# Grouping a burst's PSUM banks by their reader, and moving the norms' scalings behind dense products, in a gated HGRN2 and retention layer

## The chip, the cores and the metric

The kernel runs on one core of a Trainium2 chip. A core has five engines that run side by side, each with its own in-order queue: TensorE (PE in the profile, its weight loads PEld), VectorE (DVE), ScalarE (ACT), GpSimd (POOL) and SyncE (SP, which issues DMAs). Matmul results go to PSUM, eight banks of 128 partitions by 512 floats; the rest is in SBUF. The metric is the device time of one execution in microseconds, less is better.

## The reference

One decoder layer over 2048 positions of width 1024, in fp32. `h` is an adaptive RMS norm of `x`, one projection makes ten column groups, two recurrences run on them, their outputs are normed per head, gated and summed, and an output projection and a last norm follow:

```python
h = rms_norm(x, norm_g) * (1 + scale) + shift
hq, hf, hi, hz, rq, rk, rv, rz, ga, gb = split(h @ w_in)
oA = hgrn2_chunkwise(hq, hf, hi, lower_bounds)     # 8 heads, dk = dv = 128
uA = head_rms_norm(oA, hg_norm_g) * silu(hz)
oB = retention_chunkwise(rotary(rq), rotary(rk), rv)  # 8 heads, dk = 64, dv = 128
uB = head_rms_norm(oB, ret_norm_g) * silu(rz)
m = sigmoid(ga) * uA + sigmoid(gb) * uB
out = rms_norm(x + gate * (m @ w_out), final_g)
```

HGRN2 is `S_t = diag(f_t) S_{t-1} + (1 - f_t) i_t^T`, `o_t = S_t^T q_t` with a gate per channel; retention has one constant decay per head. Both are computed in chunks of 128 positions: a part inside the chunk (a masked score matrix times the values) and a part from the state, which every chunk updates.

## The kernel before

**Dense products.** The sequence is taken in two halves of 1024 positions. The input projection is cut into 36 quads per half (`ORDER`: a and v for HGRN2, b for retention's q and k, A and B for the gates), and each quad is seven products of a Strassen-like scheme (`product`). A product is four steps (`product_step`, j = 0 to 3) of three fp32r matmuls of 128x512. Their results lie in four PSUM banks with the tags x0, x1 and v, and are evicted by `after` at the product's end: some by ACT (`stash`, L487), some by DVE (L500 to L511). `deliver` then does the quad's own work: sigmoids, rotary (L652 to L655), gates (L693 to L707). Weights are split into two fp32r parts by ACT and DVE (L299, L300). The evictions and the splits are issued with raised priority.

**The background.** Everything else that PE does is fitted between these steps by the class `Background`. After every product step `bg.tick(1.0)` counts one tick; when eight have passed (four in one stretch of each half) `burst` advances each running generator once, in the order lanes (`hgrn_out`), rets (`retention`), trees (`tree`). `post` delays a DMA by so many ticks. `force` runs a burst at once when a tile is needed, `drain` at the end.

- `tree` builds the masked score matrix of an HGRN2 head level by level into the bank "lv" (L74 and L71), DVE multiplies factors into q and k (L814, L815, L818, L819).
- `hgrn_out` does one chunk of a head: key-value product, score times value, q times state, all into one bank "o" (`poh`, two buffers); DVE updates the state `st` from the first (L915), ACT norms the second.
- `retention` does one chunk of a pair of heads: it transposes k, multiplies the last chunk's scores with v, adds q times state, makes the next scores and the state's addition. It uses one bank "o" (`por`) and one two-bank tile "rt" (single buffer). DVE reads scores (`scm`, L1006) and state (`rs`, L1012), ACT the transposed k (`rkz`, L1009) and both outputs.
- `normed` takes the norm of an output: ACT squares with a sum (L842), POOL makes the reciprocal root (L174 or L176, then L177), ACT scales from the bank (L845). `send_u` then posts the store of u, which is fetched later for the gate, turned by PE in bank v or x (`turned_u`, the tile `uT`, L74) and multiplied (L717).

**What sets the order.** PE's instructions are pinned to program order (`InOrder`, `tc.keep_in_program_order`). For the other engines a compile-time planner picks, in simulated time, among the ready instructions the one of highest priority, which is program order except where `tc.high_priority` raises it. The order so found is each engine's queue. The planner also gives out buffers: a tile is freed when all its readers are done, and it makes accesses of one PSUM bank by different engines wait for each other in the order in which they were issued.

## Time and profile before

| What | Value |
|---|---|
| median of 3 runs (lowest, highest) | 2049.07 us (2044.88 to 2050.96) |
| the profiled execution's own time | 2047.87 us |
| its span, first to last instruction | 2046.1 us |
| PE busy | 1942.0 us, 95% |
| DVE busy | 1417.0 us, 69% |
| ACT busy | 981.2 us, 48% |
| POOL busy | 281.7 us, 14% |
| mean granted clock of TensorE | 0.987 |

A row of a group reads: line of the code, engine, operation, output and inputs by tile names, shapes, count; then busy microseconds and mean nanoseconds of one; then the idle time just before them and what ended it. A row of waits reads: who waited, for whom, microseconds in total, times, the longest. A row of a timeline reads: start, duration, engine, line, operation, tiles, count, and in brackets the idle time before and its end.

### The profile page before, as it was taken

The numbers are of one execution on the slowest core, as the hardware profiler recorded it, in microseconds if no ns is written. First come the engines' busy times: TensorE is split into PE (matmuls) and PEld (weight loads), VectorE is DVE, ScalarE is ACT, GpSimd is POOL, SyncE is SP. The second block draws the span as 40 slices with busy tenths as digits, with TensorE's granted clock in tenths as the row PEclk, the third lists the DMA queues.
The fourth block names the chain that finished last, engine by engine and source line by source line (L and its number), as shares of the span: only waits on it lengthen the run. The fifth ranks groups of instructions, "written<-read, shape, count | busy, mean of one in ns | idle before, by whom it ended". The sixth has DMA issues, their size and how long they took to land.

```text
span 2046.1 us, 40140 instructions
## 1 busy us (share of the span) xinstructions
PE 1942.0 (95%) x15172; PEld 1587.0 (78%) x15172; DVE 1417.0 (69%) x2677; ACT 981.2 (48%) x2426; POOL 281.7 (14%) x522
## 2 busy tenths in 40 slices
PE   5789899998999999999999899998999999999998
PEld 4667788877788778877888788887788878887887
DVE  6785767676767767677987676677767675868332
ACT  5524444554555446445635444534454445455331
POOL 2002110121012200201002110211011201010000
PEclk9889999999999999999999999999999999999999
DMA  8335424354353555446545424354434433246542
GB/s 296 73 89 131 123 76 113 91 140 117 106 161 117 138 138 161 148 146 200 147 109 132 124 72 109 101 148 137 115 100 126 119 86 112 73 127 191 162 144 82
DMA packets 453120, 259.96 MB, mean 127 GB/s; under 512 B 171712, under 2 KB 406208, under 8 KB 452928
## 3 DMA queue, kind: packets, MB, share of 16 engines
q1 hardware_dynamic: 286752, 172.89, 30.0%
q10 hardware_dynamic: 153120, 76.04, 13.3%
q0 software_dynamic: 13056, 8.47, 1.6%
q8 instruction: 120, 1.97, 0.4%
q14 instruction: 72, 0.59, 0.1%
HBM read 188.03 MB, written 69.21 MB: 126 GB/s over the span
## 4 chain that ended last, share of the span: by engine, by line
PE 61%; DVE 8%; DMA 7%; ACT 7%; POOL 4%; issue 3%; ACTq 1%; SPq 0%; POOLq 0%; DVEq 0%
PE x L71 25%; PE v L71 12%; PE ops L71 9%; PE y L71 6%; PE lv L71 3%; PE poh L71 2%; DVE b L300 2%; ACT b L299 2%; POOL rrh L177 1%; PE uT L74 1%; PE rt L71 1%; DVE w L425 1%; DMA wg<-in_w_gate_dram 1%; PE por L71 1%; POOL rrr L177 1%
## 5 line engine op out<-in xcount | busy, mean ns | idle before, releaser
L300 DVE TENSOR_TENSOR b<-w,b 128x512 fp32r<-128x512 f32 (+1 forms) x553 | 346.5, 634 | 291.2 <-ACT b L299 287.7
L71 PE MATMUL x<-S,b 128*128 128x512 f32 x1704 | 436.6, 401 | 9.9 <-DVE c L507 9.7
L299 ACT ACTIVATE b<-w 128x512 fp32r<-128x512 f32 (+1 forms) x553 | 316.9, 584 | 264.8 <-PE x L71 187.2
L71 PE MATMUL v<-S,b 128*128 128x512 f32 x1704 | 425.6, 398 | 4.2 <-ACT c L487 4.0
L71 PE MATMUL x<-A,b 128*128 128x512 f32 x1704 | 424.2, 397 | 3.5 <-ACT c L487 2.7
L71 PEld LDWEIGHTS v<-S,b 128*128 128x128 f32 x1704 | 317.6, 190 | 74.6 <-ACT c L487 6.4
L71 PEld LDWEIGHTS x<-A,b 128*128 128x128 f32 x1704 | 317.3, 189 | 71.4 <-ACT c L487 3.3
L71 PEld LDWEIGHTS x<-S,b 128*128 128x128 f32 x1704 | 314.9, 190 | 74.2 <-DVE c L507 7.6
L71 PE MATMUL y<-A,b 128*128 128x512 f32 x840 | 207.9, 396 | 1.9 <-DVE ro L654 1.8
L425 DVE TENSOR_TENSOR w<-w,w 128x512 f32<-128x512 f32 x284 | 194.8, 686 | 10.6 <-DMA w<-in_w_b_dram 5.4
L174 POOL TENSOR_SCALAR ssh<-ssh 128x1 f32<-128x1 f32 x128 | 49.6, 388 | 997.3 <-ACT uh L842 997.1
L71 PEld LDWEIGHTS y<-A,b 128*128 128x128 f32 x840 | 155.6, 189 | 36.2 <-issue 3.0
L71 PE MATMUL ops<-wo,m 128*128 128x512 f32 x768 | 174.5, 389 | 0.0
L71 PEld LDWEIGHTS ops<-wo,m 128*128 128x128 f32 x768 | 144.1, 188 | 29.8
L487 ACT ACTIVATE c<-v 128x512 f32<-128x512 f32 x142 | 84.6, 596 | 121.4 <-PE v L71 97.8
L845 ACT ACTIVATE uh<-poh,rrh 128x128 f32<-128x128 f32 x128 | 47.1, 368 | 154.5 <-POOL rrh L177 149.2
L71 PEld LDWEIGHTS lv<-q,k 128*32 128x32 f32 (+1 forms) x5888 | 69.8, 109 | 41.6 <-issue 30.2
L71 PE MATMUL lv<-q,k 128*32 128x16 f32 (+2 forms) x5888 | 81.0, 187 | 15.7 <-ACT af L810 5.9
L177 POOL TENSOR_TENSOR rrh<-ssh,mhalf 128x1 f32<-128x1 f32 x128 | 88.7, 693 | 10.5
L507 DVE TENSOR_TENSOR c<-c,x 128x512 f32<-128x512 f32 x71 | 48.7, 685 | 51.7 <-PE x L71 51.5
L814 DVE TENSOR_TENSOR q<-q,f 128x512 f32<-128x512 f32 x112 | 77.9, 695 | 8.2 <-PE lv L71 7.9
L815 DVE TENSOR_TENSOR k<-k,f 128x512 f32<-128x512 f32 x112 | 76.8, 686 | 0.0
(191 smaller groups left out, 2390.8 us busy)
## 6 DMA issues: line engine op xcount, KB each, us to landing
w<-in_w_d_dram ACTq DMA_DIRECT2D x128, 256.0 KB
w<-in_w_c_dram ACTq DMA_DIRECT2D x66, 256.0 KB
mu<-ud SPq DMA_DIRECT2D x64, 256.0 KB
w<-in_w_a_dram ACTq DMA_DIRECT2D x60, 256.0 KB
wa<-in_w_ada_dram SPq DMA_DIRECT2D x16, 512.0 KB
w<-in_w_b_dram ACTq DMA_DIRECT2D x32, 256.0 KB
vd<-vt SPq DMA_DIRECT2D x128, 64.0 KB
vh<-vd SPq DMA_DIRECT2D x64, 128.0 KB
```

What stands on the lines that cost most here:

```text
L71: return tc.keep_in_program_order(nc.tensor.matmul(**kw))
L74: return tc.keep_in_program_order(nc.tensor.transpose(**kw))
L174: G.tensor_scalar(out=ss, in0=ss, scalar1=n * EPS, scalar2=None, op0=ALU.add)
L177: G.tensor_tensor(out=dst, in0=ss, in1=mhalf.broadcast_to([P, w]), op=ALU.pow)
L299: S.activation(out=t[0], in_=src, func=AF.Copy)
L300: return V.tensor_tensor(out=t[1], in0=src, in1=t[0], op=ALU.subtract)
L425: V.tensor_tensor(out=out, in0=x, in1=y, op=ALU.add)
L487: S.activation(out=t, in_=ps, func=AF.Copy)
L507: V.tensor_tensor(out=t, in0=t, in1=xb[q], op=ALU.subtract)
L814: V.tensor_tensor(out=qv, in0=qv, in1=tv[:, :, :, 0:1].broadcast_to([P, NU, nb, m]), op=ALU.mult)
L815: V.tensor_tensor(out=kv, in0=kv, in1=tv[:, :, :, 1:2].broadcast_to([P, NU, nb, m]), op=ALU.mult)
L845: S.activation(out=dsts[i], in_=pos[i], func=AF.Copy, scale=rr[:, i : i + 1])
```

## The change

Each burst now has up to three PSUM tiles, shared by its generators: E and F (tag "o"), which only ACT reads, and R (tag "rt", two banks), which only DVE reads. hgrn's output goes to E, its key-value product to R; retention's transposed k and first output go to E, its second output to F (it was in "rt"), its scores and state addition to R.

The products of all generators are issued first. What reads their banks is put into a list, `bg.reads`, and issued by `flush` in the next tick (after three more dense matmuls), or at the start of the next burst. The tree's own reads stay where they were. In `normed` the squares and the root are issued with the reads, but the scalings (and the posting of u's store) go into a list `bg.scales`, due two ticks later; each scaling is also tied behind the last PE instruction issued by then (`behind`, an edge that orders the queues at compile time and adds no wait on the chip).

```diff
--- before.py
+++ after.py
+        last = None
+
+        def kept(self, ins):
+            self.last = tc.keep_in_program_order(ins)
+            return self.last
+
         def matmul(self, **kw):
...
     PE = InOrder()
     pin = tc.keep_in_program_order
+
+    def behind(ins, pe):
+        tc.add_manual_dep(
+            ins.ins, pe.ins.name, mybir.DependencyInfo(mybir.DependencyClass.NoSync, mybir.DependencyReason.DATA),
+            reason="behind",
+        )
...
+            self.reads = []
+            self.scales = []
+            self.banks = {}
+
+        def flush(self, all_=False):
+            some = bool(self.reads)
+            while self.reads:
+                self.reads.pop(0)()
+            while self.scales and (all_ or self.scales[0][0] <= self.now):
+                self.scales.pop(0)[1]()
+                some = True
+            return some
...
+        def of_act(self, k):
+            if k not in self.banks:
+                self.banks[k] = bank(f"{k}{self.nbank}", "o")
+                self.nbank += 1
+            return self.banks[k]
...
+        def of_dve(self):
+            if "R" not in self.banks:
+                self.banks["R"] = pp.tile([P, 2, 512], F32, name=f"R{self.nbank}", tag="rt", bufs=1)
+                self.nbank += 1
+            return self.banks["R"]
...
         def burst(self):
-            done = False
+            done = self.flush(True)
+            self.banks = {}
             now = self.lanes + self.rets + self.trees
...
             self.now += w
+            self.flush()
             self.deliver()
...
         def force(self):
             self.since = 0.0
             self.now += 1.0
+            self.flush(True)
             self.deliver()
...
-    def normed(pos, dsts, nm, eps=None):
...
         for i in range(n):
             S.activation(out=dsts[i], in_=pos[i], func=AF.Square, accum_out=ss[:, i : i + 1])
         rstd_of(rr[:, 0:n], ss[:, 0:n], P, eps)
-        for i in range(n):
-            S.activation(out=dsts[i], in_=pos[i], func=AF.Copy, scale=rr[:, i : i + 1])
+
+        def scale():
+            for i in range(n):
+                behind(S.activation(out=dsts[i], in_=pos[i], func=AF.Copy, scale=rr[:, i : i + 1]), PE.last)
+            then()
+
+        bg.scales.append((bg.now + 2.0, scale))
...
                 v = vs.pop(n)
-                po = bank(f"poh{h}_{gc}", "o")
+                o = bg.of_act("E")[:, 0:P]
                 sl = slice(n * P, (n + 1) * P)
+                kv = None
                 if not last:
-                    PE.matmul(out=po[:, P : 2 * P], lhsT=ktok[:, sl], rhs=v, start=True, stop=True)
-                o = po[:, 0:P]
+                    kv = bg.of_dve()[:, 0, 2 * P : 3 * P]
+                    PE.matmul(out=kv, lhsT=ktok[:, sl], rhs=v, start=True, stop=True)
                 PE.matmul(out=o, lhsT=af[:, n, :], rhs=v, start=True, stop=gc == 0)
                 if gc:
                     PE.matmul(out=o, lhsT=q[:, sl], rhs=st, start=False, stop=True)
-                if gc == 0:
-                    V.tensor_copy(out=st, in_=po[:, P : 2 * P])
-                elif not last:
-                    V.scalar_tensor_tensor(
-                        out=st, in0=st, scalar=tl[:, n : n + 1], in1=po[:, P : 2 * P], op0=ALU.mult, op1=ALU.add
+                if cc == 3 and bb == NBLK - 1:
+                    give("q")
+                    give("k")
+                    hfin[h, sb] = True
+
+                def reads(b=b, cc=cc, n=n, gc=gc, last=last, o=o, kv=kv, tl=tl, end=cc == 3 and bb == NBLK - 1):
+                    if gc == 0:
+                        V.tensor_copy(out=st, in_=kv)
+                    elif not last:
+                        V.scalar_tensor_tensor(
+                            out=st, in0=st, scalar=tl[:, n : n + 1], in1=kv, op0=ALU.mult, op1=ALU.add
+                        )
+                    if cc % 2 == 0:
+                        us_[0] = upool.tile([P, 2, P], F32, name=f"uh{h}_{b}_{cc}", tag="uh", bufs=2)
+                    u = us_[0]
+                    normed(
+                        [o], [u[:, cc % 2, :]], f"h{h}_{gc}", lambda: send_u(0, h, b, cc, u) if cc % 2 else None
                     )
-                normed([o], [u[:, cc % 2, :]], f"h{h}_{gc}")
-                if cc % 2:
-                    send_u(0, h, b, cc, u)
-                if cc == 3:
-                    if bb == NBLK - 1:
-                        give("q")
-                        give("k")
-                        hfin[h, sb] = True
+                    if end:
                         hnext[0] = (h + 1) % H
                         if not last:
                             nc.sync.dma_start(out=std[h], in_=st)
-                        else:
-                            pass
+
+                bg.reads.append(reads)
                 yield
 
...
-            pt = pp.tile([P, 2, 512], F32, name=f"rt{p}_{g0 + n}", tag="rt", bufs=1)
+            E, pt = bg.of_act("E"), bg.of_dve()
             x = pt[:, 0, P : 2 * P]
-            po = bank(f"por{p}_{g0 + n}", "o")
+            kz = E[:, 2 * P : 3 * P]
+            pos = []
             if n < CH:
...
                 vb_ = [vrs[m][:, j, :] for j in range(2)]
-                pos = [po[:, 0:P], pt[:, 1, P : 2 * P]]
+                pos = [E[:, P : 2 * P], bg.of_act("F")[:, 0:P]]
...
-            if n:
-                if not last:
+            if n and not last:
+                for j, r in enumerate(rows):
+                    PE.matmul(out=x[r, :], lhsT=kzs[m][:, r], rhs=vb_[j], start=True, stop=True)
+
+            def reads(n=n, m=m, g=g, last=last, x=x, kz=kz, pt=pt, pos=pos):
+                if n < CH:
+                    scms[n] = upool.tile([P, 2, P], F32, name=f"scm{p}_{g0 + n}", tag="scm", bufs=1)
+                    V.tensor_tensor(
+                        out=scms[n], in0=pt[:, :, 0:P], in1=dT.rearrange("p (j t) -> p j t", j=2), op=ALU.mult
+                    )
+                    kzs[n] = upool.tile([P, P], F32, name=f"rkz{p}_{g0 + n}", tag="rkz", bufs=1)
                     for j, r in enumerate(rows):
-                        PE.matmul(out=x[r, :], lhsT=kzs[m][:, r], rhs=vb_[j], start=True, stop=True)
-            if n < CH:
-                scms[n] = upool.tile([P, 2, P], F32, name=f"scm{p}_{g0 + n}", tag="scm", bufs=1)
-                V.tensor_tensor(out=scms[n], in0=pt[:, :, 0:P], in1=dT.rearrange("p (j t) -> p j t", j=2), op=ALU.mult)
-                kzs[n] = upool.tile([P, P], F32, name=f"rkz{p}_{g0 + n}", tag="rkz", bufs=1)
-                for j, r in enumerate(rows):
-                    S.activation(out=kzs[n][:, r], in_=kz[:, r], func=AF.Copy, scale=zeta[:, h0 + j : h0 + j + 1])
-            if n:
+                        S.activation(out=kzs[n][:, r], in_=kz[:, r], func=AF.Copy, scale=zeta[:, h0 + j : h0 + j + 1])
+                if not n:
+                    return
                 if g and not last:
...
-                normed(pos, [u[j][:, m % 2, :] for j in range(2)], f"r{p}_{g}", epsx[:, h0 : h0 + 2])
-                if m % 2:
-                    for j in range(2):
-                        send_u(1, h0 + j, b, m % 4, u[j])
+                us_ = [u[0], u[1]]
+
+                def then():
+                    if m % 2:
+                        for j in range(2):
+                            send_u(1, h0 + j, b, m % 4, us_[j])
+
+                normed(pos, [z[:, m % 2, :] for z in us_], f"r{p}_{g}", then, epsx[:, h0 : h0 + 2])
...
+            bg.reads.append(reads)
             n += 1
             yield
```

More of the change, by code (lines that the diff above doesn't have):

```diff
@@ L68, in tile_hybrid @@
     class InOrder:
+        last = None
+        def kept(self, ins):
+            self.last = tc.keep_in_program_order(ins)
+            return self.last
         def matmul(self, **kw):
-            return tc.keep_in_program_order(nc.tensor.matmul(**kw))
+            return self.kept(nc.tensor.matmul(**kw))
         def transpose(self, **kw):
-            return tc.keep_in_program_order(nc.tensor.transpose(**kw))
+            return self.kept(nc.tensor.transpose(**kw))
     PE = InOrder()
     pin = tc.keep_in_program_order
+    def behind(ins, pe):
[3 more added lines that the diff above has]
+        )
     cpool = ctx.enter_context(tc.tile_pool(name="cpool", bufs=1))
@@ L201, in __init__ @@
             self.posts = []
+            self.reads = []
[19 more added lines that the diff above has]
+            return self.banks["R"]
+        nbank = 0
         def burst(self):
-            done = False
+            done = self.flush(True)
+            self.banks = {}
             now = self.lanes + self.rets + self.trees
@@ L264, in drain @@
             for _ in range(4000):
-                if not (self.rets or self.trees or self.lanes or self.side or self.posts):
+                if not (self.rets or self.trees or self.lanes or self.side or self.posts or self.reads or self.scales):
                     return
@@ L835, in tree, with normed @@
             us[h, sb * NBLK + bb] = (q, kk, tl, f0, bg.now)
-    def normed(pos, dsts, nm, eps=None):
+    def normed(pos, dsts, nm, then, eps=None):
         n = len(pos)
@@ L859, in hgrn_out @@
             nc.sync.dma_start(out=st, in_=std[h])
-        vs, age = {}, {}
+        vs, age, us_ = {}, {}, [None]
         def fetch(n):
@@ L892, in hgrn_out @@
             for cc in range(4):
-                if cc % 2 == 0:
-                    u = upool.tile([P, 2, P], F32, name=f"uh{h}_{b}_{cc}", tag="uh", bufs=2)
                 n = 4 * bb + cc
@@ L978, in retention @@
             last = g == L // P - 1
-            pt = pp.tile([P, 2, 512], F32, name=f"rt{p}_{g0 + n}", tag="rt", bufs=1)
+            E, pt = bg.of_act("E"), bg.of_dve()
             x = pt[:, 0, P : 2 * P]
-            po = bank(f"por{p}_{g0 + n}", "o")
+            kz = E[:, 2 * P : 3 * P]
+            pos = []
             if n < CH:
-                kz = po[:, P : 2 * P]
                 PE.transpose(out=kz, in_=qks[n][:, 1, :], identity=ident)
```

## The prediction, made before the result was known

> **What bounds the kernel now.** I read the page first: its busy times and the chain of waits.
>
> ```profile
> span 2046.1 us, 40140 instructions
> PE 1942.0 (95%) x15172; PEld 1587.0 (78%) x15172; DVE 1417.0 (69%) x2677; ACT 981.2 (48%) x2426; POOL 281.7 (14%) x522
> PE 61%; DVE 8%; DMA 7%; ACT 7%; POOL 4%; issue 3%; ACTq 1%; SPq 0%; POOLq 0%; DVEq 0%
> ```
>
> TensorE (PE) is busy 95% of the span, so what can be won without removing products is at most its idle time, 2046.1 - 1942.0 = 104.1 us. The chain that ended last runs 61% on PE. The change removes no product, so I ask which of PE's waits it can reach. The view of PE's waits (who waited for whom; us in total, times, longest) has these rows that concern the background's products, the turned u (uT) or the dense products around them; the opening's waits (row of c, first h) are left out, because the change does not touch them.
>
> ```profile
> PE uT L74 <- ACT c L487: 12.3, 9, 2.3
> ...
> PE lv L71 <- ACT af L810: 5.9, 2, 4.2
> PE lv L71 <- DVE k L818: 5.5, 4, 2.0
> ...
> PE poh L71 <- DVE st L915: 4.9, 6, 1.8
> PE rt L71 <- ACT ur L845: 4.5, 4, 1.8
> PE v L71 <- ACT c L487: 4.0, 5, 2.3
> ...
> PE x L71 <- ACT c L487: 2.7, 2, 2.0
> PE lv L71 <- DVE k L815: 2.5, 2, 2.3
> ...
> PE por L74 <- ACT ur L845: 1.7, 2, 1.1
> ```
>
> Three causes stand there: ScalarE (ACT) evicts a bank too late (12.3 + 4.0 + 2.7 = 19.0 us), a norm's scaling frees a bank too late (4.5 + 1.7 = 6.2 us), and VectorE (DVE) is late with the tree's factors or the state (5.5 + 2.5 + 4.9 = 12.9 us). Next the waits of ACT, an engine that is only 48% busy:
>
> ```profile
> ACT uh L845 <- POOL rrh L177: 149.2, 124, 4.4
> ...
> ACT uh L842 <- DVE st L915: 77.8, 68, 5.1
> ACT ur L845 <- POOL rrr L177: 63.5, 59, 1.9
> ```
>
> ACT stands still 149.2 + 63.5 = 212.7 us in front of scalings (L845) whose root POOL has not finished, and 77.8 us in front of squares (L842) that must wait until DVE has read the same bank. Its queue is in order, so an eviction behind such a scaling waits too. The timeline around 410 us shows how this reaches PE:
>
> ```profile
> 409.82 0.28 ACT L842 ACTIVATE uh<-poh 128x128 f32<-128x128 f32 x1 [1.29 <-DVE st L915]
> 409.99 0.20 ACT L842 ACTIVATION_READ_ACCUMULATOR uh<-poh 128x1 f32 x1
> ...
> 411.63 0.37 ACT L845 ACTIVATE uh<-poh,rrh 128x128 f32<-128x128 f32 x1 [1.19 <-POOL rrh L177]
> ...
> 413.34 0.37 ACT L845 ACTIVATE ur<-por,rrr 128x128 f32<-128x128 f32 x1 [1.09 <-POOL rrr L177]
> ...
> 413.86 0.60 ACT L487 ACTIVATE c<-v 128x512 f32<-128x512 f32 x1
> ...
> 414.51 0.66 PE L74 MATMUL uT<-ident,mu 128*128 128x128 f32 x4 [1.26 <-ACT c L487]
> ```
>
> ACT lost 1.29 + 1.19 + 1.09 us, then evicted the bank v, and PE, which needed v for uT, lost 1.26 us.
>
> **The change, part by part.** No matmul, DMA, square, root or scaling is added or removed, and PE's order (hgrn's products, retention's, the tree's) stays. So the sum is made of waits alone.
>
> *ACT's and DVE's reads in separate banks.* The squares no longer wait for st (77.8 us of ACT idle). This is off PE's path except through ACT's queue; it is priced with the next part.
>
> *The scalings two ticks behind the reads, and behind PE's dense products.* A tick is three dense matmuls. Twelve of them start 2.72 us apart from the next twelve:
>
> ```profile
> 1002.85 2.68 PEld L71 LDWEIGHTS v<-S,b 128*128 128x128 f32 x12
> ...
> 1005.57 2.68 PEld L71 LDWEIGHTS x<-A,b 128*128 128x128 f32 x12
> ```
>
> A tick is therefore 2.72/4 = 0.68 us. Reads are issued one tick after the burst and scalings at the earliest two later, 3 x 0.68 = 2.04 us after the burst. How long the root takes, from the groups by line:
>
> ```profile
> L177 POOL TENSOR_TENSOR rrh<-ssh,mhalf 128x1 f32<-128x1 f32 x128 | 88.7, 693 | 10.5
> ...
> L174 POOL TENSOR_SCALAR ssh<-ssh 128x1 f32<-128x1 f32 x128 | 49.6, 388 | 997.3 <-ACT uh L842 997.1
> L177 POOL TENSOR_TENSOR rrr<-ssr,mhalf 128x2 f32<-128x2 f32 x64 | 49.5, 774 | 5.0
> ...
> L1009 ACT ACTIVATE rkz<-por,zeta 128x64 f32<-128x64 f32 x128 | 33.1, 310 | 14.0 <-PE rt L71 5.8 <-DVE rs L1012 2.7 <-issue 2.1
> ...
> L176 POOL TENSOR_TENSOR ssr<-ssr,epsx 128x2 f32<-128x2 f32 x64 | 17.1, 268 | 244.7 <-ACT ur L842 244.7
> ```
>
> For hgrn: square and accumulator read 0.28 + 0.20, POOL 0.39 + 0.69, together 1.56 us, less than 2.04: that wait (149.2 us of ACT idle) goes when ACT takes the square at once. For retention: hgrn's square 0.48, two rkz 0.62, two more squares 0.96, then POOL 0.27 + 0.77: 3.10 us, 1.06 more than 2.04, which is today's 63.5/59 = 1.08. So I keep retention's wait and drop hgrn's, 149.2/212.7 = 70% of the standstill. Of PE's 19.0 us behind late evictions I give up not 70% (13.3) but half, **9.5 us**, because some evictions are late behind plain work in the queue. Bounds: 0 and 19.0.
>
> *Banks freed by the scalings.* Banks E and F (two "o" buffers) are held to the scaling as now, but "rt" (single) is freed by DVE and no longer by ACT, and ACT reaches the scaling with fewer stalls in front. Of the 6.2 us I take away **5.2** and leave 1.0 for a burst whose scaling comes late. Bounds: 0 and 6.2 won here; the loss is the third rival.
>
> *The tree's DVE work ahead of the state's.* In a burst with a tree step the reads are now issued behind the tree's factors, so these (L814, L815, L818) start earlier by at least one state update of 0.34 us (a row of the next fence). For the 6 waits of 8.0 us on k: 6 x 0.34 = **2.0 us** won. Bounds: 0 and 8.0.
>
> *hgrn's key-value product now writes R.* R has one buffer, read by DVE alone, and this product is the first of the burst. So DVE's reads of the last burst must be done before the first product instead of the third, and they stand one tick later in the issue order, where dense evictions' follow-ups (gate, rotary) can come ahead. The tightest place in the trace is the stretch with bursts every four ticks:
>
> ```profile
> 920.04 0.38 PE L71 MATMUL poh<-vh,k 128*128 128x128 f32 x2
> ...
> 921.38 0.69 DVE L698 TENSOR_TENSOR sz<-x,sz 128x512 f32<-128x512 f32 x1 [2.68 <-ACT sz L693]
> 921.99 0.68 DVE L300 TENSOR_TENSOR b<-w,b 128x512 fp32r<-128x512 f32 x1
> 922.59 0.69 DVE L700 TENSOR_TENSOR c<-c,sz 128x512 f32<-128x512 f32 x1
> 923.19 0.34 DVE L915 SCALAR_TENSOR_TENSOR st<-st,tl,poh 128x128 f32<-128x128 f32 x1
> ...
> 923.90 0.38 PE L71 MATMUL poh<-vh,k 128*128 128x128 f32 x2
> ...
> 924.35 0.39 PE L71 MATMUL poh<-st,q 128*128 128x128 f32 x2
> ```
>
> The update ends at 923.53, 0.37 us ahead of the next key-value product and 0.82 ahead of the product that needs it today. For the 6 updates that are late already (4.9 us) I add 924.35 - 923.90 = 0.45 us for the earlier need and one more DVE operation of 0.69: 6 x 1.14 = **6.8 us** lost. Bounds: 0 (DVE gets its splits sooner, because ACT halves them without standing still) and 28, the second rival. In full bursts there is room: st at 1310.91 stands 1317.85 - 1311.25 = 6.6 us ahead of its next burst.
>
> ```profile
> 1301.45 3.02 PE L71 MATMUL v<-S,b 128*128 128x512 f32 x12
> ...
> 1305.69 0.36 ACT L845 ACTIVATE ur<-rt,rrr 128x128 f32<-128x128 f32 x1
> ...
> 1307.70 0.27 PE L74 MATMUL por<-ident,rqk 128*128 128x128 f32 x1
> ...
> 1310.91 0.34 DVE L915 SCALAR_TENSOR_TENSOR st<-st,tl,poh 128x128 f32<-128x128 f32 x1
> ...
> 1317.85 0.38 PE L71 MATMUL poh<-vh,k 128*128 128x128 f32 x2
> ```
>
> *DMAs.* The stores of u on SP are issued behind the scalings, so at most some 2 us later; the retention's next rows (rqk) and the v rows pass them on the same queue. On ACT's queue the issues of the weights' loads come ahead of the scalings now and lose their standstill. u is fetched many products later, so I price this at nothing; if that cover is gone, a late u adds its lateness to uT.
>
> **Sum.** -9.5 - 5.2 - 2.0 + 6.8 = -9.9 us against the profiled execution's 2047.9 us (span 2046.1 and 1.8 around it): 2038.0. The median of the three runs, 2049.07, lies 1.2 us above that execution, so I predict **2039 us**.
>
> **Rivals.** *The stall only moves.* A burst after a product's first step has its scalings fall due exactly at that product's last step, before its eviction; retention's root is then still 1.06 us away, and the eviction stands behind it as at 413.34. Then the 9.5 us stay, and 5.2 + 2.0 - 6.8 = 0.4 us is won: 2049. For it speaks that the rows at 413.34 and 414.51 are of retention; against, that hgrn has 149.2 of the 212.7 us.
>
> *R becomes the bound (slower).* If the reads of one in four of the 112 state updates fall behind two gate operations, 2 x 0.69 - 0.37 = 1.01 us of PE is lost each time, 28 us; less the 16.7 won, the time is 2049 + 11 = 2060. It decides from some 17 such updates on, where its price passes the gains. For it: DVE is busy 69%, and the margin of 0.37 us. Against: most updates have several us, as at 1310.91.
>
> *Banks held longer (slower).* At 1306.05 the last scaling ends, 1.65 us ahead of the next burst's first write to a retention bank at 1307.70. If scalings came 2.04 us later than today, PE would wait 0.39 us in each of 64 retention steps, 25 us in place of the 5.2 won: 2039 + 5 + 25 = 2069. Against: today's scaling at 1305.69 already starts 4.24 us after the dense products that follow its burst (1301.45), so the new floor of 2.04 us does not bind. The Trainium skill (page "PSUM — Partial Sum Buffer", section "Summary: rules for kernel authors") speaks for this rival: it advises to evacuate banks promptly, and the change holds them on purpose. The 6.2 us of waits on L845 agree that late release costs here, but at 7 places only.
>
> **Chances.** The forecast 0.50, the stall that moves (and a change without effect) 0.27, R as the bound 0.15, banks held longer 0.08. The forecast's own range is 2028 to 2047: without the 6.8 us of loss and with 4 us more of the late evictions at the low end, with the 16.7 us of gains halved at the high end. To leave out no more than 2 in 10 the range must take in the second case and the nearer slower one: 2026 to 2061. A change under 0.3% (6 us) cannot be told from none here; so faster 0.50, same 0.27, slower 0.23.
>
> **What would show it.** Right: ACT's wait on rrh (149.2 us) falls below 40 us, its wait on st (77.8 us) disappears, PE's waits of uT on c fall to under 6 us, those of rt and por on L845 to about 1 us. Retention's wait on rrr stays near 60 us. The price shows as a wait of hgrn's key-value product on st or on another DVE read of R, near 12 us in all. Wrong: if these ACT waits go and PE's idle time stays near 104 us, the evictions were late for another reason; if PE waits more than 25 us on DVE's reads, R is the bound.

## The result, and the profile after

The changed kernel takes 2019.84 us (median of 4 runs, 2015.04 to 2021.59). The kernel before, beside it, takes 2047.76 (2044.88 to 2050.96). The ratio is 0.986, with an interval of 0.9836 to 0.9883: 28 us less. I had forecast 2039, some 10 us less, with a range from 2026 up. The direction is right; the size is nearly three times the forecast, and the time lies below the range.

The head of the page of the changed kernel:

```profile
span 2013.3 us, 40043 instructions
...
PE 1930.3 (96%) x15172; PEld 1581.7 (79%) x15172; DVE 1420.3 (71%) x2677; ACT 985.7 (49%) x2426; POOL 296.6 (15%) x522
```

PE is idle for 2013.3 - 1930.3 = 83.0 us, against 104.1 before. PE is also busy 11.7 us less, though it does the same 15172 matmuls. The chain that ended last is no measure here: it lies 61% on PE in the first profile of the kernel before and 82% in the changed one, but in a second profile of the kernel before the chain that could be followed covers only 11% of the span.

This profiled execution took 2015.04 us, the lowest of the four. A second profile of the changed kernel (2019.97 us, near the median) and a second one of the kernel before (2047.99 us) stand beside the first ones below. The line of busy times of the changed kernel's second page:

```profile
PE 1934.8 (96%) x15172; PEld 1585.4 (79%) x15172; DVE 1419.9 (70%) x2677; ACT 987.7 (49%) x2426; POOL 294.7 (15%) x522
```

PE's waits in the changed kernel, first profile (who waited for whom; us in total, times, longest). L528 is the old eviction L487, L888 the scaling L845, L966 the state update L915, L856 and L859 the tree's factors L815 and L818:

```profile
PE R L77 <- DVE st L966: 8.8, 3, 4.7
...
PE lv L77 <- DVE k L856: 5.6, 3, 3.0
...
PE lv L77 <- DVE k L859: 3.7, 3, 2.0
PE uT L80 <- ACT c L528: 3.4, 2, 2.9
...
PE E L77 <- ACT ur L888: 2.7, 2, 2.1
PE v L77 <- ACT c L528: 2.4, 3, 1.3
PE E L80 <- ACT ur L888: 1.8, 3, 0.9
PE lv L77 <- ACT ur L888: 1.5, 1, 1.5
PE F L77 <- ACT ur L888: 0.9, 2, 0.7
```

Some of the waits of the kernel before were not in my sum, because their named releaser is neither an eviction nor a scaling. These are the wait of lv on af (5.9, shown in the prediction) and four more:

```profile
PE uT L74 <- DVE sz L698: 3.9, 2, 3.2
...
PE y L71 <- DVE ro L654: 1.8, 1, 1.8
PE por L74 <- DMA rqk<-rd: 1.7, 1, 1.7
...
PE lv L71 <- ACT rb L1059: 1.5, 1, 1.5
```

A wait carries the name of what came last, and the name can change while the wait stays. The tree's products into lv show it. This is the same product of the tree in the kernel before and in the changed one:

```profile
1156.43 1.12 PE L71 MATMUL lv<-q,k 128*64 128x64 f32 x16 [4.19 <-ACT af L810]
...
1129.46 0.69 PE L77 MATMUL lv<-q,k 128*64 128x64 f32 x16 [3.04 <-DVE k L856]
```

So 4.19 us under the name of af became 3.04 us under the name of k. In the same way lv's wait of 1.76 us on af at 255.35 became the 1.5 us of lv on ur at 247.88; no scaling reads lv's bank. The account of PE's idle time therefore takes all waits of lv together. It is in us, from these rows and their counterparts in the other two profiles:

| PE waits for | before | before again | changed | changed again | forecast change |
|---|---|---|---|---|---|
| a late eviction (uT, v, x on c) | 19.0 | 18.8 | 5.8 | 4.2 | -9.5 |
| a bank held by a scaling (rt, por; now E, F) | 6.2 | 6.7 | 5.4 | 4.5 | -5.2 |
| the tree's reads and factors (lv, on whatever name) | 15.4 | 15.9 | 11.7 | 11.3 | -2.0 |
| the state update (poh on st; now R on st) | 4.9 | 4.2 | 8.8 | 9.6 | +6.8 |
| sz, ro, rqk (left out of the sum) | 7.4 | 5.3 | 1.6 | 2.4 | 0 |
| the rest (opening, output, small waits) | 51.2 | 53.3 | 49.7 | 51.4 | 0 |
| PE's idle time in all | 104.1 | 104.2 | 83.0 | 83.4 | -9.9 |

The second profile of the changed kernel is 2047.87 - 2019.97 = 27.9 us shorter than the first of the kernel before: 20.7 of it is idle time and 7.2 is busy time (1942.0 to 1934.8). Part of the busy time lies ahead of anything that the change touches. The tree's first product starts at 114.83 us in the kernel before and at 110.53 in the changed one, with 76.9 and 72.7 us of PE busy until then; the first norm follows more than 50 us later. So 4.2 of the 7.2 us are there already. In the second profile of the kernel before that product starts at 113.31, in the first of the changed one at 109.93, and in the profiles of the variants below (without the two with added stops) between 107.84 and 112.63.

ACT's waits for the roots in the changed kernel:

```profile
ACT uh L888 <- POOL rrh L189: 97.4, 87, 3.3
...
ACT ur L888 <- POOL rrr L189: 51.6, 55, 1.7
```

The standstill on rrh was to fall from 149.2 to under 40 us and fell to 97.4 only. Counted from ACT's timeline, 88 of the 128 scalings of hgrn stood directly behind their own square in ACT's queue before, and 51 still do; these 51 hold 65.4 of the 97.4 us. That on rrr was to stay near 60 and is 51.6. The wait of 77.8 us for the state update in front of the squares is gone, as forecast. So 70% of ACT's standstill in front of scalings is still there, and PE's waits behind late evictions went all the same. The timeline around 400 us, the same stretch of work that the prediction showed around 410, says why:

```profile
400.43 0.28 ACT L883 ACTIVATE uh<-E 128x128 f32<-128x128 f32 x1 [0.53 <-PE F L77]
...
401.48 0.56 POOL L189 TENSOR_TENSOR rrh<-ssh,mhalf 128x1 f32<-128x1 f32 x1
...
402.07 0.37 ACT L888 ACTIVATE uh<-E,rrh 128x128 f32<-128x128 f32 x1
...
403.55 0.37 ACT L888 ACTIVATE ur<-E,rrr 128x128 f32<-128x128 f32 x1 [1.11 <-POOL rrr L189]
...
404.68 0.60 ACT L528 ACTIVATE c<-v 128x512 f32<-128x512 f32 x1 [0.51 <-PE v L77]
...
406.31 0.60 PE L80 MATMUL uT<-ident,mu 128*128 128x128 f32 x4
```

The squares of both recurrences stand together, so hgrn's root is made while ACT squares retention's outputs, and uh is scaled at 402.07 without a wait. Of the three waits that cost 1.29 + 1.19 + 1.09 us before, only that for retention's root is left, 1.11 us. The eviction of v at 404.68 now waits for PE (0.51 us), not for the queue in front of it, and uT at 406.31 follows without a wait where it lost 1.26 us.

The new price stands where I had put it, on R. The timeline of the worst of the three waits:

```profile
1346.63 0.25 ACT L883 ACTIVATE uh<-E 128x128 f32<-128x128 f32 x1
...
1354.04 0.68 DVE L341 TENSOR_TENSOR b<-w,b 128x512 fp32r<-128x512 f32 x1
...
1354.64 0.69 DVE L695 TENSOR_TENSOR c<-c,ct 128x512 f32<-128x512 f32 x1
...
1355.24 0.34 DVE L966 SCALAR_TENSOR_TENSOR st<-st,tl,R 128x128 f32<-128x128 f32 x1
...
1355.64 0.79 PE L77 MATMUL R<-vh,k 128*128 128x128 f32 x2 [4.69 <-DVE st L966]
```

ACT squared this burst's output at 1346.63. The state update from the same burst came 8.6 us later, behind splits (L341) and rotary operations (L695). The second rival had named gate operations, but the mechanism is its own. It happens at 3 places, not at the 17 from which that rival decides.

### The profile page after: what moved, and what is told of

It is laid out like the page before. It is cut to its first block, busy times and chain, and to the rows that moved or that the text cites. A ratio compares the mean times of both kernels' runs of the same rounds, so it can differ in the third digit from the quotient of the medians.

```text
span 2013.3 us, 40043 instructions
## 1 busy us (share of the span) xinstructions
PE 1930.3 (96%) x15172; PEld 1581.7 (79%) x15172; DVE 1420.3 (71%) x2677; ACT 985.7 (49%) x2426; POOL 296.6 (15%) x522
## 3 DMA queue, kind: packets, MB, share of 16 engines
q10 hardware_dynamic: 153120, 76.04, 13.4%
## 4 chain that ended last, share of the span: by engine, by line
PE 82%; DMA 8%; DVE 5%; ACT 2%; issue 1%; POOL 1%; SPq 1%; ACTq 0%; POOLq 0%; DVEq 0%
PE x L77 33%; PE v L77 17%; PE ops L77 9%; PE y L77 8%; PE E L77 4%; PE lv L77 3%; PE R L77 3%; PE uT L80 2%; DMA rd<-c 1%; DMA ud<-ur 1%; DVE b L341 1%; DVE w L466 1%; PE F L77 1%; DMA sn<-lin 1%; ACT b L340 1%
## 5 line engine op out<-in xcount | busy, mean ns | idle before, releaser
L341 DVE TENSOR_TENSOR b<-w,b 128x512 fp32r<-128x512 f32 (+1 forms) x553 | 346.8, 635 | 228.1 <-ACT b L340 219.5
L186 POOL TENSOR_SCALAR ssh<-ssh 128x1 f32<-128x1 f32 x128 | 51.2, 400 | 999.5 <-ACT uh L883 999.4
L528 ACT ACTIVATE c<-v 128x512 f32<-128x512 f32 x142 | 84.6, 596 | 149.6 <-PE v L77 134.4
L888 ACT ACTIVATE uh<-E,rrh 128x128 f32<-128x128 f32 x128 | 47.3, 369 | 111.6 <-POOL rrh L189 97.4
L189 POOL TENSOR_TENSOR rrh<-ssh,mhalf 128x1 f32<-128x1 f32 x128 | 97.7, 763 | 10.6
L528 ACT ACTIVATE c<-y 128x512 f32<-128x512 f32 x70 | 41.8, 597 | 73.7 <-PE y L77 73.6
```

Source lines behind the costliest of these rows:

```text
L186: G.tensor_scalar(out=ss, in0=ss, scalar1=n * EPS, scalar2=None, op0=ALU.add)
L189: G.tensor_tensor(out=dst, in0=ss, in1=mhalf.broadcast_to([P, w]), op=ALU.pow)
L341: return V.tensor_tensor(out=t[1], in0=src, in1=t[0], op=ALU.subtract)
L528: S.activation(out=t, in_=ps, func=AF.Copy)
L888: behind(S.activation(out=dsts[i], in_=pos[i], func=AF.Copy, scale=rr[:, i : i + 1]), PE.last)
```

## The experiments

All ratios are to the kernel before, run on the same chip; "beside it" is that kernel's median there. The intervals of the ratios reach 0.001 to 0.002 to each side, 2 to 4 us.

| kernel | banks E, F, R | reads a tick later | scalings later | time, us | beside it | ratio and interval | PE idle | PE busy |
|---|---|---|---|---|---|---|---|---|
| before again | no | no | no | 2049.76 | 2048.97 | 1.0006 (0.9995 to 1.0018) | 104.2 | 1942.0 |
| scalings alone | no | no | yes | 2032.04 | 2045.43 | 0.9931 (0.9913 to 0.9948) | 92.6 | 1939.2 |
| banks alone | yes | no | no | 2037.10 | 2048.97 | 0.9943 (0.9925 to 0.9961) | 94.5 | 1944.0 |
| scalings at once | yes | yes | no | 2034.94 | 2045.43 | 0.9947 (0.9928 to 0.9966) | 93.4 | 1938.2 |
| banks as before | no | yes | yes | 2033.51 | 2045.43 | 0.9933 (0.9915 to 0.9950) | 91.5 | 1939.6 |
| reads at once | yes | no | yes | 2027.14 | 2045.43 | 0.9908 (0.9892 to 0.9924) | 89.1 | 1938.5 |
| changed again | yes | yes | yes | 2019.94 | 2046.98 | 0.9864 (0.9845 to 0.9882) | 83.4 | 1934.8 |

**The kernel before and the changed one again.** Nothing is edited; the first is a second profile of the kernel before.

> The kernel before once more, for a second profile of it: 2041 to 2051 us. If the first 140 us are about 4 us shorter than in its first profile, that part of the difference to the changed kernel is one execution's clock and no effect of the change; if they are as long as there, the change reaches the opening, which no step of the prediction does. PE's idle time should be 100 to 106 us again.

> The changed kernel itself, on the chip of the next three, as their measure: 2013 to 2023 us, 1.2 to 1.6 per cent under the kernel before.

Both agree with the first runs: 1.0006 (no difference) and 0.9864 against 0.986. PE's idle time repeats to 0.4 us in both kernels, and PE's busy time in the kernel before is 1942.0 both times. So the idle time of one profile can be compared between kernels, though a single row of waits moves by up to 2 us (uT on sz is 3.9 and 1.9 in the two profiles of the kernel before). A busy time differs by 4.5 us between two executions of the changed kernel. The opening of the kernel before is 1.5 us shorter in its second profile, against 4.3 and 4.9 in the changed one; whether the rest is the execution or the change is not settled.

**Scalings alone.** The kernel before, with its banks and reads as they were; only the scalings go into the list, due three ticks after the burst. The list, `behind` and `flush` are those of the change; the central lines are:

```diff
...
         rstd_of(rr[:, 0:n], ss[:, 0:n], P, eps)
-        for i in range(n):
-            S.activation(out=dsts[i], in_=pos[i], func=AF.Copy, scale=rr[:, i : i + 1])
+
+        def scale():
+            for i in range(n):
+                behind(S.activation(out=dsts[i], in_=pos[i], func=AF.Copy, scale=rr[:, i : i + 1]), PE.last)
+            then()
+
+        bg.scales.append((bg.now + 3.0, scale))
...
```

> The kernel before with its banks and its reads, but the scalings three ticks after the burst and behind PE's dense products. Theory 1: ScalarE's wait on rrh falls to 100 us or less, and 60 to 80 per cent of the gain is there, 2025 to 2031 us; the waits of squares on the state update (78 us) stay. Theory 2: 2040 to 2050 us, since the banks are the old ones. A third effect, the two-bank tile rt held longer by the later scaling, would show as PE waits on L845's successor over 15 us and a time above 2050 us.

Measured: 0.9931, 13.4 us less: half of the gain, a little above the window of the first theory. One row of ACT's waits, then rows of PE's:

```profile
ACT uh L864 <- DVE st L942: 69.7, 65, 5.1
```

```profile
PE uT L80 <- ACT c L509: 5.8, 3, 2.6
...
PE v L77 <- ACT c L509: 4.4, 4, 2.3
...
PE x L77 <- ACT c L509: 2.6, 1, 2.6
```

The late evictions fall from 19.0 to 12.8 us, ACT's standstill on rrh from 149.2 to 111.9. ACT still waits 69.7 us for DVE in front of its squares.

**Banks alone.** The changed kernel with the reads issued at the burst's end and the scalings right behind the root:

```diff
                 now = again
+            while self.reads:
+                self.reads.pop(0)()
             return done
...
-        def scale():
-            for i in range(n):
-                behind(S.activation(out=dsts[i], in_=pos[i], func=AF.Copy, scale=rr[:, i : i + 1]), PE.last)
-            then()
-
-        bg.scales.append((bg.now + 2.0, scale))
+        for i in range(n):
+            S.activation(out=dsts[i], in_=pos[i], func=AF.Copy, scale=rr[:, i : i + 1])
+        then()
```

> The kernel with the banks E, F and R alone: reads at the end of their burst, scalings at once with them. If the three parts add up (scalings alone gave 13 us, banks with deferred reads 10, banks with delayed scalings 18), banks alone give about 5 us, 2039 to 2044 us. If the banks need the later issue of the reads to be of use, nothing or a loss, 2044 to 2052 us. If the banks carry what the tick of delay seemed to carry, 10 us or more, under 2037 us.

Measured: 0.9943, 11.9 us less. Among ACT's waits the row of the squares on st is gone, and the standstill on rrh is what it was before (149.2); a row of PE's waits follows:

```profile
ACT uh L889 <- POOL rrh L189: 148.6, 122, 2.8
```

```profile
PE uT L80 <- ACT c L530: 5.9, 6, 1.7
```

So the banks' order is worth about as much as the scalings' delay, the third case of the expectation. I had put it off PE's path "except through ACT's queue" and priced it with the other part; that queue is where it pays: uT's wait on c falls from 12.3 to 5.9 us, and late evictions in all (with 3.0 of v and 1.2 of x) from 19.0 to 10.1, with the standstill on the roots untouched. PE's waits for banks that a scaling holds fall to 0.8 us. The two parts add up: late evictions fall by 8.9 us with the banks alone, by 6.2 with the scalings alone, and by 13.2 and 14.8 in the changed kernel.

**Scalings at once.** The changed kernel with the last edit of the one above only (reads deferred, scalings right behind the root).

> The changed kernel with its banks E, F and R and its deferred reads, but each norm's scaling issued right behind its root, with the reads, as before the change. Theory 1 (ScalarE's standstill in front of scalings makes evictions late, and PE waits): ScalarE's wait on rrh is back near 149 us, PE's waits of uT, v and x on evictions near 19 us, and the time is 2038 to 2046 us. Theory 2 (the banks grouped by reader carry the gain): the time stays at 2018 to 2026 us, although the standstill on rrh is back. Theory 3 (the planner merely found a luckier order): the time lies anywhere from 2015 to 2055 us with no relation to the standstill.

Measured: 0.9947, 10.5 us less, which the intervals do not tell from banks alone. With the new banks, deferring the reads adds nothing without the scalings' delay. Neither of the first two theories holds as it was put: ACT's standstill on rrh is back (150.9 us), but PE's late evictions come to 5.1 (uT) + 1.9 (v) + 1.3 (x) = 8.3 us and not to 19, and the time lies between the two windows. R costs 9.4 us on st and 5.5 that the profile calls issue.

**Banks as before.** The changed kernel with the old bank of hgrn and the old "por" and "rt" of retention; reads and scalings come as late as in the changed kernel:

```diff
-                o = bg.of_act("E")[:, 0:P]
+                po = bank(f"poh{h}_{gc}", "o")
+                o = po[:, 0:P]
...
-                    kv = bg.of_dve()[:, 0, 2 * P : 3 * P]
+                    kv = po[:, P : 2 * P]
...
-            E, pt = bg.of_act("E"), bg.of_dve()
+            pt = pp.tile([P, 2, 512], F32, name=f"rt{p}_{g0 + n}", tag="rt", bufs=1)
+            po = bank(f"por{p}_{g0 + n}", "o")
             x = pt[:, 0, P : 2 * P]
-            kz = E[:, 2 * P : 3 * P]
+            kz = po[:, P : 2 * P]
...
-                pos = [E[:, P : 2 * P], bg.of_act("F")[:, 0:P]]
+                pos = [po[:, 0:P], pt[:, 1, P : 2 * P]]
```

> The changed kernel with deferred reads and delayed scalings, but the PSUM banks of before (one o bank per hgrn chunk and per retention step, rt read by both engines). Theory 1: near the changed kernel, 2020 to 2028 us, squares wait about 78 us on the state update again. Theory 2: most of the gain is gone, 2038 to 2050 us.

Measured: 0.9933, 11.9 us less, between the two theories; the squares wait 52.7 us on the state update again. Here the third rival shows itself in part. PE's waits for banks that a scaling holds:

```profile
PE por L80 <- ACT ur L888: 6.0, 4, 3.4
...
PE rt L77 <- ACT ur L888: 4.3, 4, 1.4
...
PE poh L77 <- ACT uh L888: 1.4, 2, 0.8
```

They come to 11.7 us, nearly twice the 6.2 before. The delay of the scalings is not enough to explain that: in "scalings alone", with the same old banks and scalings due at the same time, such waits are 2.4 (rt) + 1.3 (por) = 3.7 us. It takes the deferred reads as well, and why is open. With E and F the waits are 5.4 and 4.5 in the changed kernel, and 0.8 with the banks alone. So the new banks do win the 5.2 us that I counted, and the later reads and scalings give most of it back.

**Reads at once.** The changed kernel with the first edit of "banks alone", and the scalings due three ticks after the burst as before (`bg.now + 3.0`).

> The changed kernel, but the reads of E, F and R are issued at the end of their burst instead of one tick later; the scalings fall due at the same time as in the changed kernel (three ticks after the burst). If the tick of delay of the reads carries nothing, 2017 to 2024 us. If the delay delays the state update (PE's wait of R on st, 8.8 us), this one is faster, 2010 to 2016 us. If issuing dense evictions ahead of the reads is what made evictions early, it is slower, 2026 to 2036 us, with uT's wait on c back above 8 us.

Measured: 0.9908, 18.3 us less, 8.7 us short of the 27.0 of the changed kernel in its own group of runs. PE's idle time is 5.7 us more than in the changed kernel's second profile. The time falls into the window of the third case, but the sign of that case is missing: late evictions are 4.0 (uT) + 2.7 (v) us. What is worse are two waits of dense products for a split made by DVE, a row that is 0.9 us in the first profile of the changed kernel and absent in the second; the wait of R on st is shorter (6.7 us). Two rows of DVE's timeline follow:

```profile
PE v L77 <- DVE b L343: 4.7, 1, 4.7
...
PE x L77 <- DVE b L343: 3.4, 1, 3.4
```

```profile
724.39 0.69 DVE L1127 TENSOR_TENSOR xT<-xT,rb 128x512 f32<-128x512 f32 x1 [9.88 <-DMA xT<-in_x_t_dram]
725.00 0.68 DVE L343 TENSOR_TENSOR b<-w,b 128x512 fp32r<-128x512 f32 x1
```

The split that v needs stands in DVE's queue behind an operation on xT that waits 9.88 us for its DMA. The other split, at 1372.72, stands behind one that waits 6.08 us for wg's. So it is not the reads of R that delay these splits, but operations that wait for their loads. That the tick of delay is worth 8.7 us in itself is not shown.

**No edge behind PE.** The changed kernel with plain scalings in place of those tied behind PE's last instruction (`behind(...)` taken away).

> The changed kernel without the edges that tie each scaling behind a PE instruction; the two ticks of delay in the issue order stay. If the edges carry the delayed scalings (the planner, which thinks the root is quick, would otherwise draw them forward), ScalarE's wait on rrh is back at 130 to 150 us and the time is like that with scalings at once, 2026 to 2036 us. If the issue order alone holds them back, nothing changes: 97 us of that wait and 2015 to 2022 us.

Measured: 2023.94 us beside 2046.98, ratio 0.9889 (0.9870 to 0.9909); PE idle 87.6 us, ACT's wait on rrh 103.4. That is 4 us more than the changed kernel, with intervals that overlap, and between the two cases of the expectation: the edges add at most a few us, and the delay of the issue does the rest.

**Scalings due four ticks after the reads.** `bg.now + 2.0` becomes `bg.now + 4.0`.

> The changed kernel with scalings due four ticks after the reads instead of two (2.7 instead of 1.4 us). By the standstill theory the 97 us of wait on rrh and the 52 us on rrr fall to a third or less, and PE's waits on evictions (uT, v on c: 5.8 us) nearly vanish, 2010 to 2018 us. By the rival that banks are held too long, PE's waits of E and F on the scalings (5.4 us) grow to 15 us or more, and in the stretch with bursts every four ticks the scalings are forced out before the next burst anyway: 2022 to 2035 us.

Measured: 2021.77 us, ratio 0.9881 (0.9863 to 0.9899). A row of ACT's waits in this kernel, and one of PE's:

```profile
ACT uh L888 <- POOL rrh L189: 3.3, 4, 1.9
```

```profile
PE E L77 <- ACT ur L888: 5.2, 6, 4.3
```

ACT's standstill on rrh is gone, 94 us of it, no scaling of hgrn stands directly behind its square any more, and the kernel is no faster. The forecast of 2010 to 2018 us failed. Late evictions fall from 4.2 to 2.2 us and lv's waits from 11.3 to 9.9, but PE waits longer for banks that the scalings hold (7.2 us instead of 4.5; E's products 5.2 instead of 2.7) and 2.5 us in front of R. So the standstill left in the changed kernel costs little, some 3 us, and taking it away costs at least as much elsewhere. ACT's idle time in front of scalings was the wrong measure; the right one is what PE needs from behind them.

**State update raised.** The update of st from R is issued at the priority of the evictions:

```diff
-                    if gc == 0:
-                        V.tensor_copy(out=st, in_=kv)
+                    with tc.high_priority(offset=PEV):
+                        if gc == 0:
+                            V.tensor_copy(out=st, in_=kv)
...
```

> The changed kernel with the hgrn state update (VectorE's read of R) at the evictions' raised priority. If R is a bound on the path, PE's wait of R on st (8.8 us) goes to under 3 us and the time falls by 5 to 9 us against the changed kernel. If that wait is only VectorE's backlog moved about, another VectorE wait (lv on k, x on c) grows by as much and the time is within 4 us of the changed kernel.

Measured: 2024.39 us, ratio 0.9887 (0.9872 to 0.9902). The wait on R falls, and others rise by as much:

```profile
PE v L77 <- ACT c L528: 5.8, 4, 2.7
PE uT L80 <- ACT c L528: 5.7, 3, 2.9
...
PE R L77 <- DVE st L967: 2.5, 2, 2.0
```

R's 9.6 us become 2.5, the evictions' 4.2 become 12.5 (with 1.0 of x) and uT's wait on sz rises from 1.9 to 3.7. PE's idle time is 87.3 us. Not only DVE's waits grew, as the second case had it, but those for ACT's evictions. The price on R can be moved, and here it was not worth moving.

**Stops of PE, long and short.** To see what a stop costs, the changed kernel gets 24 added stops in dense products: a small matmul, a chain of ACT copies, and a matmul that needs the last copy. These are extra work that the layer does not need. The chain is eight copies in the one kernel and one in the other; nothing else differs.

```diff
...
+            if j == 2 and 60 <= i < 300 and i % 10 == 0:
+                with tc.high_priority(offset=FIRSTS):
+                    ps_ = bank(f"stall{i}", "lv")
+                    PE.matmul(out=ps_[0:32, 0:32], lhsT=ones[:, 0:32], rhs=ident[:, 0:32], start=True, stop=True)
+                    S.activation(out=stall[0:32, 0:32], in_=ps_[0:32, 0:32], func=AF.Copy)
+                    for _ in range(7):    # range(0) in the short one
+                        S.activation(out=stall, in_=stall, func=AF.Copy)
+                    PE.matmul(out=ps_[0:32, 32:64], lhsT=ones[:, 0:32], rhs=stall[:, 0:32], start=True, stop=True)
```

> The changed kernel with 24 extra stops of PE between dense matmuls: a small matmul, a chain of eight ScalarE copies on it, and a small matmul that needs the last. Estimated from rows of such copies, PE idles 2 to 3 us each time, 50 to 75 us in all. If a stop costs its idle time and no more, the time grows by that idle time within a tenth. If a stop of that length also brings stretches at half the granted clock, as behind the stops at 243 us and 1153 us in the profile before, it grows by 1.2 to 1.7 times the idle time and the records of half clock grow by 40 us or more.

> The same 24 stops with one ScalarE copy each, about 1 us of idle time. If half clock follows only from stops of some 2 us and more, the time grows by the added idle time alone, some 20 to 30 us, and the records of half clock stay at 20 to 40 us. If every stop brings it, they grow by 40 us here too.

Measured, beside 2048.97: 2143.68 us (ratio 1.0463, 1.0442 to 1.0484) with long stops and 2050.11 (1.0001, 0.9990 to 1.0012) with short ones. PE is busy 1983.4 us with the long stops and 1952.4 with the short ones, in 15268 matmuls each. PE's wait on the stops, first of the long, then of the short:

```profile
PE stall L77 <- ACT stall L585: 91.0, 24, 8.7
```

```profile
PE stall L77 <- ACT stall L583: 23.0, 24, 6.6
```

The two have the same PE instructions. The long stops add 93.6 us of time: PE's idle time rises by 62.4 (95.9 to 158.3) and its busy time by 31.0. So a us of idle time in long stops costs 1.5 us, as the second case of the expectation had it. Against the changed kernel the short stops show no clear surcharge: some 28 us of time by the two ratios (1.0001 against 0.9864), of which 12.5 are idle time and some 13 the 96 added matmuls (24 times a pair of 0.25 and a pair of 0.31 us). What is left, 2 us by the ratios and 4 by the profiles, is no more than two executions of one kernel differ.

## Why the prediction was right or wrong

**Right: the mechanism and the direction.** PE's waits behind late evictions fell, because ACT's queue lost standstills in front of them: the scalings' delay and the banks' order, each alone, lower them by 6.2 and 8.9 us. ACT's wait for st went; the number of PE's instructions stayed the same; R brought a new wait on the state update; retention's root still costs its 1.1 us. The wait of uT on c was to fall under 6 us and is 3.4 and 3.5.

**Wrong: the sum.** It came to -9.9 us and the times moved by 28. The steps, by the account above (first profile of the kernel before, second of the changed one):

- *Late evictions, -9.5: the step that failed most.* Measured -14.8 (19.0 to 4.2). I took half of these waits, starting from the 70% of the scalings' standstill that was to go. The squares' wait of 77.8 us for st was "priced with the next part" and then got no price of its own: that part counts only the waits in front of scalings. The banks alone, which end that wait and leave the one on rrh at 148.6, take 8.9 of these 19.0 us.
- *Banks freed by scalings, -5.2.* Measured -1.7. The new banks alone bring it (6.2 to 0.8), and the later reads and scalings, which I gave no price here, hold the banks again.
- *The tree's products, -2.0.* Measured -4.1, taking lv's waits together. Those under the name of k did not fall (8.0 to 8.9), because a wait that had been named after af now has that name.
- *R, +6.8.* Measured +4.7; "near 12 us in all" is 8.8 and 9.6. The term was right in kind and somewhat too large.
- *Nothing for sz, ro and rqk.* Measured -5.0 (-2.9 from the second profile of the kernel before). I had left them out because their releaser is no eviction and no scaling. That they went because of the standstills is argued and not shown.
- *PE's busy time as a constant.* I set the most that could be won equal to the idle time and let busy time stand. It is 7.2 us less (11.7 in the lower execution), of which 4.2 stand ahead of the tree's first product, where the change has not acted yet. Whether any of it is the change stays open; see the last section.

So the 27.9 us between the two profiled executions are 20.7 of idle time, where the sum had 9.9, and 7.2 of busy time, where it had none. With the idle time alone the forecast would have been about 2028.

**The forecast of hgrn's standstill (149.2 to under 40) failed** by its size: 1.56 us of work against a floor of 2.04 was to clear it, and 97.4 us remained, 87 waits of 1.1 us. The floor was counted in ticks of issue, and ACT's queue did not keep it: 51 scalings still follow their square with nothing between. Reading at once and scaling three ticks later, 2.04 us by my tick, left 94.9 us. Only at four ticks after the reads did it go (3.3 us), and that brought no gain in time.

**The rivals.** *The stall only moves*: not so for the whole change, but it is what happens when one more wait is attacked (the raised state update, the four ticks). *R becomes the bound*: its mechanism is there, at 3 places instead of 28. *Banks held longer*: the Trainium skill (page "PSUM — Partial Sum Buffer", section "Summary: rules for kernel authors") advises to evacuate banks promptly. The runs agree in part: waits for banks that scalings hold came to 11.7 us with the old banks, delayed scalings and deferred reads, but to 3.7, under the 6.2 of the kernel before, with the scalings' delay alone. With E and F they are 5.4 and 4.5. Those 6.2 us stand at 6 places in the prediction's rows, not at 7.

**The parts together.** Gains over the kernel before, in us: scalings alone 13.4, banks alone 11.9, both without deferred reads 18.3, all three 27.0. PE's idle time falls by 11.5, 9.6, 15.0 and 20.7. Deferred reads give nothing on top of the banks alone (10.5) or on top of the scalings alone (11.9 with them), and 9 on top of both, where two splits of DVE stand behind operations that wait for a load. How much of these 9 us is deferral, and how much the order that the planner happened to find, is open; no run separates them.

None of the variants is faster than the changed kernel.

## What to carry to other kernels

In an in-order queue, don't price a standstill by its own length, but by what stands behind it. List all waits of the bounding engine on any instruction of that queue, whatever name the releaser has, and compare two kernels wait by wait at the same waiting instruction: the name can change while the wait stays. A long-latency pair (square, root on another engine, scaling) is best cut in two with unrelated work between, and PSUM banks are best shared only by readers of one engine, so that no engine waits for another's read; here each alone gave some 12 us and the two with deferred reads 27. When results are held longer on purpose, look for the wait to come back as a bank that is not free.

## What the runs showed of the hardware

The granted clock of TensorE goes to one half for stretches, and stops of PE bring it there. In the kernel with long stops, the timeline of PE around its longest stop and a window of 2 us behind it (the third number from the end of a window's row is the granted clock):

```profile
507.11 1.62 PE L77 MATMUL y<-A,b 128*128 128x512 f32 x6 [0.46 <-DVE ro L706]
...
517.64 0.31 PE L77 MATMUL stall<-stall,ones 128*32 128x32 f32 x2 [8.73 <-ACT stall L585]
517.88 2.89 PE L77 MATMUL y<-A,b 128*128 128x512 f32 x6
```

```profile
518.00:520.00 2.00, 2.00 (x5) 1.62 (x6) 0.00 (x0) 0.00 (x0) 0.00 (x0) 0.50 0.14 48
```

Six dense matmuls take 1.62 us before the stop and 2.89 behind it, at a clock of 0.50. The mean clock of this kernel's profiled execution is 0.963, against 0.983 with short stops, and PE is busy 31.0 us more for the same matmuls. In windows of 2 us, from 100 us to 60 us before the end, the clock is under 0.75 in 63 windows with long stops and in 25 with short ones; it is so in 17 and 22 windows of the two profiles of the kernel before and in 10 and 20 of the changed one. The Trainium skill (page "TensorE: Matmul & The Clock Gate", section "HAM oscillation — how this bites in real kernels") gives as a rule that no idle gap of PE should exceed some 3.4 us. The long stops, 91.0/24 = 3.8 us in the mean, agree. But in the kernel before, a burst behind a wait of 1.70 us is already followed by a stretch at half clock; PE's timeline and a window of it:

```profile
243.68 0.33 PE L74 MATMUL por<-ident,rqk 128*128 128x128 f32 x1 [1.70 <-DMA rqk<-rd]
...
246.82 4.00 PE L71 MATMUL x<-A,b 128*128 128x512 f32 x12
```

```profile
246.00:248.00 2.00, 2.00 (x70) 1.62 (x68) 1.97 (x5) 0.94 (x5) 0.00 (x0) 0.50 0.68 142
```

The same twelve matmuls take 3.01 us in the changed kernel, where the wait for rqk is gone:

```profile
237.69 3.01 PE L77 MATMUL x<-A,b 128*128 128x512 f32 x12
```

With the banks alone, a wait of 1.04 us for rqk and one of 0.28 for vr at that place are followed by the same twelve matmuls in 4.21 us. So waits shorter than the rule's can be followed by half clock here, and there the measurement decides; whether the single wait brings it, or what PE did around it as well, is not shown. Nor is the half clock saved for good: in the changed kernel a wait of 2.12 us for a held bank follows at 242.82, and the clock is 0.50 from 244 to 248 us.

So a wait can cost more than its idle time. It is not shown that this carries any of the change's 7.2 us of busy time: the mean clock of an execution was 0.980 to 0.992 in the runs of the kernel before and 0.982 to 0.993 in those of the changed one, which is no difference. Nor do the profiles give one price of the clock. The two busy times of the changed kernel (1930.3 at a clock of 0.993, 1934.8 at 0.988) lie 0.9 us apart for each 0.001, the two kernels with stops 1.5, and the kernel before was busy 1942.0 us at 0.987 and at 0.983 alike.
